# Two transformer blocks on one core: conditioning sums along rows of a transposed weight, the first activations in tiles of their own, the last output in three pieces

## The chip, the cores and the metric

The kernel runs on one core of a Trainium2 chip. The metric is the device time of one execution in microseconds (us). Comparisons are medians of several executions; one further execution is taken with the hardware profiler on, and all rows below come from it.

## What is computed

A sequence of 256 rows of width 1024 goes through a first block of two layers (feed-forward, mixer, feed-forward, each with a residual and a layer norm) and then through a second block of two layers, whose input and output are modulated by a conditioning vector `c`. Cut to what the change touches:

```
def swiglu_ffn(x, w_gu, w_down):
    a, u = jnp.split(x @ w_gu, 2, axis=-1)
    return (jax.nn.silu(a) * u) @ w_down

# second block, layer l; c is (1, 1024), w_ada[l] is (1024, 3072)
mod = jax.nn.silu(c) @ w_ada[l] + b_ada[l]
shift, scale, gate = jnp.split(mod, 3, axis=-1)
h = x * (1.0 + scale[:, None, :]) + shift[:, None, :]
...
x = layer_norm_2(ALPHA * x + (1.0 + gate[:, None, :]) * sub, ln_g[l], ln_b[l])
```

## The kernel before, in words

All matmuls work on fp32 numbers that are split into two parts: `hilo` (lines 375 to 378) and `get_at` (294 to 304) let ScalarE (ACT) write a rounded high part (`xx`, `whi`, `xhi`, `hth`) and VectorE (DVE) the rest as a low part (`wlo`, `xlo`, `htl`). A product then takes three matmuls, high by high, low by high and high by low.

The weights come from memory as a stream of pieces of 128 rows by up to 1024 columns, in the order in which `plan` (64 to 116) lists them. `load_piece` (280 to 286) issues each on the SP queue into one of six staging tiles `st` (NS = 6); a tile is free again when DVE has made the low part of its piece. The split pieces lie in eight pairs `whi`, `wlo` (NB = 8) or in tiles `xhi`, `xlo` of the stage. A stage's instructions are written in program order, and each engine runs its own list in order.

A feed-forward stage runs over 22 chunks of 128 hidden columns. `gu_T` (520 to 546) makes the gate and up products of a chunk: for each of 8 k tiles (128 rows of the weight) and both halves, one matmul of 512 columns with `whi` as weights and high and low activations side by side as moving data, and one of 256 columns with `wlo`: 16 such pairs a chunk. Even chunks write the two PSUM banks `mm`, odd chunks the two banks `tr`; DVE's additions at line 541 free the banks. `down` adds the product of chunk c - 6 to four banks `ac`.

The start of the kernel is special. `setup` clears part of `x` and `warm` (222 to 229) runs 18 matmuls on it. The first feed-forward takes its activations transposed from memory in four pieces of two k tiles (`load_xT`, 231 to 236), which go through the same staging tiles and the same SP queue as the weights, between the pieces of chunk 0 (`FIRST_K`, line 27). The identity `idn` for transposes is loaded by the POOL queue.

The modulation is worked out beside the feed-forward stages. 48 pieces of `w_ada` lie in the stream, eight for each of six groups of 1024 outputs (`ADA`, line 30: one group in the first, two in the second, two in the third, one in the fourth feed-forward stage). In `ada_step` (306 to 327) a piece holds 128 inputs on partitions and 1024 outputs on columns. DVE multiplies it by the partition's `silu(c)` and adds it to `ada` (lines 315 and 317). After the eighth piece the partitions still have to be summed: TensorE transposes `ada` in two groups of four blocks of 128 columns (`transposes`, 441 to 447) into a bank `tr`, and DVE sums each group along its rows (line 324).

At the end `ln` (400 to 429) writes each half of 128 rows in two pieces of 512 columns, both issued on SP.

Of the kernel before, what the change touches and what calls it, by code (L numbers as in the profile page):

```python
# [17 lines left out]
D = 1024  # L18
# [8 lines left out]
FIRST_K = ((0, 1), (1, 1), (2, 2), (4, 2), (6, 2))  # L27
# [36 lines left out]
def plan(take):  # L64
# [6 lines left out]
    def ffn(i, l):  # L71
# [47 lines left out]
def lay_out(inp):  # L119
    d = {}  # L120
    f = lambda a: np.ascontiguousarray(a)
    src = {**inp, "w_ukv": np.concatenate([inp["w_uk_2"], inp["w_uv_2"]], 2), "w_out_2": inp["w_out_2"][:, Y2]}
# [7 lines left out]
    d["xT"] = f(inp["x"][0].T.reshape(4, 2, 128, 2, 128).transpose(0, 2, 3, 1, 4).reshape(4, 128, 512))  # L130
    d["bada"] = f(inp["b_ada_2"].reshape(DEPTH * 24, 128).T)
    d["c"] = f(inp["c_2"].reshape(8, 128).T)
# [50 lines left out]
class Kernel:  # L183
# [12 lines left out]
    def setup(self):  # L196
# [9 lines left out]
        self.c = self.const.tile([128, 8], F32, name="c")  # L206
        self.sc = self.const.tile([128, 8], F32, name="sc")
        self.mod = [self.const.tile([128, 24], F32, name=f"mod{l}") for l in range(DEPTH)]
        nc.gpsimd.dma_start(out=self.idn, in_=d["idn"])
# [4 lines left out]
        nc.scalar.activation(out=self.sc, in_=self.mhalf, func=AF.Silu)  # L214
# [4 lines left out]
        self.n_ox = 0  # L219
        self.warm()  # L220
# [10 lines left out]
    def load_xT(self, q):  # L231

        st = self.stage.tile([128, 1024], F32, name="st")[:, :512]
        self.nc.sync.dma_start(out=st, in_=self.d["xT"][q])
        ks = slice(2 * q, 2 * q + 2)
        self.hilo(self.xh[:, :, ks, :], self.xl[:, :, ks, :], st.rearrange("p (t k n) -> p t k n", t=2, k=2))

    def load_x(self, c):

        if c == 7:  # L240
# [5 lines left out]
            self.nc.sync.dma_start(out=self.c, in_=self.d["c"])  # L246
            self.nc.scalar.activation(out=self.sc, in_=self.c, func=AF.Silu)
# [6 lines left out]
    def open_block1(self):  # L254
# [5 lines left out]
        self.dec = p.tile([128, 2048], F32, name="dec")  # L260

# [44 lines left out]
    def ada_step(self, pool):  # L306

        nc = self.nc
        while self.pieces and self.pieces[0][0] == "a":
            _, l, k, _, cols = self.pieces[0][3]  # L310
            st = self.load_piece()[1]
            c = self.sc[:, k:k + 1]
            if k == 0:
# [1084 lines left out]
```

## Time and profile before

| | |
|---|---|
| time, median of three runs | 1345.4 us (1343.68 to 1346.33) |
| the profiled execution, its own time | 1350.96 us |
| span in that profile, first to last instruction | 1349.2 us |
| matmuls, TensorE busy | 7654, 1319.8 us (98%) |
| VectorE busy, ScalarE busy | 1031.4 us (76%), 741.4 us (55%) |
| moved by DMA | 262.88 MB |

PE is TensorE's matmuls, DVE is VectorE, ACT is ScalarE, SPq is the queue on which SP issues DMAs. Times of rows count from the span's start. A busy PE is not PE at its peak, since matmuls are pipelined: what a group of them costs is read from start to start. In a timeline row the first number is the start, the second the time that the row covers, `x4` the number of instructions in it, and the bracket holds the idle time before it and who ended that. `PEclk` is the granted clock of TensorE.

### The profile page before, as it was taken

To read this page: it belongs to the slowest core of one execution; us is meant where nothing else is said; L and a number is where in the kernel's file an instruction comes from. 1 tells how busy PE (TensorE), PEld (TensorE's weight loads), DVE (VectorE), ACT (ScalarE), POOL (GpSimd) and SP (SyncE) were. 2 spreads that over 40 slices of the span, in tenths; PEclk is the share of its full clock that TensorE was granted. 3 is DMA by queue.
4 is the path that set the end of the run, shared out by engine and by line. 5 is a ranking of instruction groups with operands and counts; after the bars stand their busy time and mean duration, and the time that the engine had idled before them with its cause. 6 is when DMAs were issued, how large, how long until landed. Compare 5 with 4: busy or idle time off the path is not lost. (4 is left out here: it accounts for less than half of the span.)

```text
span 1349.2 us, 20437 instructions
## 1 busy us (share of the span) xinstructions
PE 1319.8 (98%) x7654; PEld 1135.5 (84%) x7654; DVE 1031.4 (76%) x1713; ACT 741.4 (55%) x1310; POOL 25.8 (2%) x35
## 2 busy tenths in 40 slices
PE   8999999999999999999999999999999999999997
PEld 6888888788887888888887878888889998799886
DVE  6876769968977669787579878687585797866976
ACT  6654536446655546545446456555355678456681
POOL 0000000010000000000000110000000000000000
PEclk9999999999999999999999999999999999999999
DMA  8987724546878628877423637677445433464420
GB/s 290 332 297 234 240 93 133 203 134 232 316 244 268 212 83 305 299 255 250 156 96 125 252 124 269 202 260 265 131 151 184 154 126 128 138 203 160 143 77 32
DMA packets 75235, 262.88 MB, mean 195 GB/s; under 512 B 9168, under 2 KB 9552, under 8 KB 75008
## 3 DMA queue, kind: packets, MB, share of 16 engines
q1 hardware_dynamic: 74592, 259.82, 56.9%
q0 software_dynamic: 544, 1.75, 0.4%
q8 instruction: 60, 0.98, 0.3%
q14 instruction: 39, 0.32, 0.1%
HBM read 260.49 MB, written 1.05 MB: 194 GB/s over the span
## 5 line engine op out<-in xcount | busy, mean ns | idle before, releaser
L302 DVE TENSOR_TENSOR wlo<-st,whi 128x1024 fp32r<-128x1024 f32 (+4 forms) x319 | 372.3, 1176 | 74.6 <-ACT whi L300 73.1
L300 ACT ACTIVATE whi<-st 128x1024 fp32r<-128x1024 f32 (+4 forms) x319 | 322.6, 1021 | 123.4 <-PE mm L331 49.6
L331 PE MATMUL mm<-xx,whi 128*128 128x256 f32 (+1 forms) x1296 | 335.0, 334 | 1.2 <-DVE xx L378 1.2
L331 PE MATMUL mm<-xx,wlo 128*128 128x256 f32 x928 | 262.1, 283 | 0.0
L331 PEld LDWEIGHTS mm<-xx,whi 128*128 128x128 f32 x1296 | 221.0, 191 | 25.7 <-ACT whi L300 1.5
L331 PE MATMUL mm<-whi,xx 128*128 128x512 f32 (+3 forms) x744 | 219.1, 372 | 0.6 <-DVE xx L378 0.4
L331 PE MATMUL tr<-xx,whi 128*128 128x512 f32 x560 | 197.3, 394 | 2.2 <-ACT whi L300 2.2
L331 PEld LDWEIGHTS mm<-xx,wlo 128*128 128x128 f32 x928 | 176.8, 191 | 2.2 <-DVE wlo L302 0.5
L331 PE MATMUL tr<-xx,wlo 128*128 128x256 f32 x560 | 157.6, 282 | 0.5 <-DVE wlo L302 0.5
L331 PEld LDWEIGHTS mm<-whi,xx 128*128 128x128 f32 x744 | 135.0, 188 | 24.5 <-issue 1.6
L302 DVE TENSOR_TENSOR xlo<-st,xhi 128x1024 fp32r<-128x1024 f32 x106 | 128.4, 1219 | 26.0 <-ACT xhi L300 26.0
L300 ACT ACTIVATE xhi<-st 128x1024 fp32r<-128x1024 f32 x106 | 110.2, 1056 | 67.6 <-PE ac L331 56.3
L331 PE MATMUL mm<-wlo,xx 128*128 128x512 f32 (+3 forms) x372 | 137.0, 369 | 0.0
L331 PEld LDWEIGHTS tr<-xx,whi 128*128 128x128 f32 x560 | 105.4, 188 | 26.0 <-ACT whi L300 2.6
L331 PE MATMUL ac<-xlo,hth 128*128 128x512 f32 x320 | 126.2, 394 | 0.0
L331 PE MATMUL ac<-xhi,hth 128*128 128x512 f32 x320 | 125.4, 392 | 0.0
L331 PEld LDWEIGHTS tr<-xx,wlo 128*128 128x128 f32 x560 | 106.5, 190 | 2.2 <-DVE wlo L302 1.0
L331 PE MATMUL ac<-xhi,htl 128*128 128x512 f32 x320 | 105.0, 392 | 0.0
L317 DVE SCALAR_TENSOR_TENSOR ada<-st,sc,ada 128x1024 f32<-128x1024 f32 x42 | 53.8, 1281 | 41.5 <-DMA st<-in_w 41.5
L331 PEld LDWEIGHTS mm<-wlo,xx 128*128 128x128 f32 x372 | 70.1, 188 | 10.6 <-issue 0.3
L331 PEld LDWEIGHTS ac<-xhi,hth 128*128 128x128 f32 x320 | 60.1, 188 | 14.1
L331 PEld LDWEIGHTS ac<-xhi,htl 128*128 128x128 f32 x320 | 60.0, 188 | 12.4
(275 smaller groups left out, 1823.1 us busy)
## 6 DMA issues: line engine op xcount, KB each, us to landing
st<-in_w SPq DMA_DIRECT2D x442, 512.0 KB, 4.6
st<-in_w SPq DMA_DIRECT2D x20, 384.0 KB, 3.7
g<-in_lng SPq DMA_DIRECT2D x8, 512.0 KB, 4.8
b<-in_lnb SPq DMA_DIRECT2D x8, 512.0 KB, 5.2
st<-in_w SPq DMA_DIRECT2D x8, 432.0 KB, 4.1
st<-in_w SPq DMA_DIRECT2D x8, 296.0 KB, 3.9
st<-in_xT SPq DMA_DIRECT2D x4, 256.0 KB, 4.5
x<-in_x SPq DMA_DIRECT2D x2, 512.0 KB, 7.7
```

Source lines behind the costliest of these rows:

```text
L300: nc.scalar.activation(out=hi[:, :m], in_=st[:, :m], func=AF.Copy)
L302: nc.vector.tensor_tensor(out=lo[:, :m], in0=st[:, :m], in1=hi[:, :m].bitcast(F32), op=ALU.subtract)
L317: nc.vector.scalar_tensor_tensor(out=self.ada, in0=st, scalar=c, in1=self.ada, op0=ALU.mult, op1=ALU.add)
L331: return self.nc.tensor.matmul(*a, **k).ins
```

## The change

There are four edits.

1. `w_ada` is laid out transposed. A piece now holds 128 outputs on partitions and all 1024 inputs on columns. `silu(c)` is spread over all partitions as a tile `sc` of 128 by 1024. One DVE instruction for each piece multiplies and sums along the row (`accum_out`) straight into a column of `mod`. The products and transposes on TensorE, the tile `ada` and the sums at line 324 are gone. The 48 pieces stay where they were in the stream.
2. The activations `xx` are laid out by k tile, for each k the 256 high columns and then the 256 low ones (`xk`). The first activations no longer go through staging tiles: they land in `x[1]`, in the upper half of `x[0]` and in a temporary tile. The first piece is issued in two halves of one k tile on the ACT queue, ahead of everything else on it; the other three stay on SP.
3. Chunk 1 takes its weights in three pieces (2, 2 and 4 k tiles) in place of two. `idn` and the broadcast `c` (512 KB) are loaded on SP behind chunk 7, with `x`.
4. The last output is written in pieces of 512, 384 and 128 columns; the middle one is issued on the ACT queue.

```diff
-FIRST_K = ((0, 1), (1, 1), (2, 2), (4, 2), (6, 2))
+FIRST_K = (((0, 1), (1, 1), (2, 2), (4, 2), (6, 2)), ((0, 2), (2, 2), (4, 4)))
...
-            for k, kk in FIRST_K if start and c == 0 else ((0, 4), (4, 4)):
+            for k, kk in FIRST_K[c] if start and c < 2 else ((0, 4), (4, 4)):
...
-                yield piece("a", "w_ada_2", al, k, 1, rng(1024 * q, 1024))
+                yield piece("a", "w_ada_T", al, 8 * q + k, 1, rng(0, 1024))
...
-        nc.gpsimd.dma_start(out=self.idn, in_=d["idn"])
...
-        self.xx = self.xt.tile([128, 2, 2, 8, 128], F32R, name="xx")
-        self.xh, self.xl = self.xx[:, 0], self.xx[:, 1]
-        self.xhl = self.xx.rearrange("p e t k n -> p (e t) k n")
+        self.xk = self.xt.tile([128, 8, 512], F32R, name="xx")
+        self.xh, self.xl = (self.xk[:, :, c:c + 256].rearrange("p k (t n) -> p t k n", t=2) for c in (0, 256))
...
+        self.xw = self.tmp()
+        for k in range(2):
+            nc.scalar.dma_start(out=self.x[1][:, 256 * k:256 * k + 256], in_=d["xT"][0][:, 256 * k:256 * k + 256])
...
-    def load_xT(self, q):
-        st = self.stage.tile([128, 1024], F32, name="st")[:, :512]
-        self.nc.sync.dma_start(out=st, in_=self.d["xT"][q])
-        ks = slice(2 * q, 2 * q + 2)
-        self.hilo(self.xh[:, :, ks, :], self.xl[:, :, ks, :], st.rearrange("p (t k n) -> p t k n", t=2, k=2))
+    def load_xT(self, k, n):
+        q, r = divmod(k, 2)
+        src = (self.x[1][:, 0:512], self.x[1][:, 512:], self.x[0][:, 512:], self.xw)[q][:, 256 * r:256 * (r + n)]
+        if q > 0:
+            self.nc.sync.dma_start(out=src, in_=self.d["xT"][q])
+        self.hilo(self.xk[:, k:k + n, :256], self.xk[:, k:k + n, 256:], src.rearrange("p (k n) -> p k n", k=n))
...
-            self.nc.sync.dma_start(out=self.c, in_=self.d["c"])
-            self.nc.scalar.activation(out=self.sc, in_=self.c, func=AF.Silu)
+            self.nc.sync.dma_start(out=self.idn, in_=self.d["idn"])
+            self.nc.sync.dma_start(out=self.sc, in_=self.d["c"].to_broadcast([128, D]))
+            self.nc.scalar.activation(out=self.sc, in_=self.sc, func=AF.Silu)
...
-            if k == 0:
-                self.ada = pool.tile([128, 1024], F32, tag="ada", name="ada", bufs=2)
-                nc.vector.tensor_scalar(out=self.ada, in0=st, scalar1=c, scalar2=None, op0=ALU.mult)
-            else:
-                nc.vector.scalar_tensor_tensor(out=self.ada, in0=st, scalar=c, in1=self.ada, op0=ALU.mult, op1=ALU.add)
-            if k < 7:
+            nc.vector.scalar_tensor_tensor(out=st, in0=st, scalar=1.0, in1=self.sc, op0=ALU.mult, op1=ALU.mult,
+                                           accum_out=self.mod[l][:, j:j + 1])
+            if j % 8 < 7:
                 continue
...
-            for h in range(2):
-                ps = self.transposes([self.ada[:, 512 * h + 128 * i:512 * h + 128 * i + 128] for i in range(4)])
-                nc.vector.tensor_reduce(out=m[:, 4 * h:4 * h + 4], in_=ps.rearrange("p (k n) -> p k n", k=4), axis=AX.X,
-                                        op=ALU.add)
...
-            for c0, c1 in HALVES:
+            for c0, c1, q in ((0, 512, nc.sync), (512, 896, nc.scalar), (896, 1024, nc.sync)):
                 nc.vector.scalar_tensor_tensor(out=x[:, c0:c1], in0=x[:, c0:c1], scalar=y, in1=self.b[:, c0:c1],
                                                op0=ALU.mult, op1=ALU.add)
-                nc.sync.dma_start(out=self.out[128 * t:128 * t + 128, c0:c1], in_=x[:, c0:c1])
+                q.dma_start(out=self.out[128 * t:128 * t + 128, c0:c1], in_=x[:, c0:c1])
...
-                    K.mm(o, lhsT=hi[:, i, cs], rhs=K.xhl[:, :, k, :], start=k == 0, stop=False, skip_group_check=True)
+                    K.mm(ps[j], lhsT=hi[:, i, cs], rhs=K.xk[:, k, :], start=k == 0, stop=False, skip_group_check=True)
```

What the edits do to the order of the instructions shows at three places. On SP, the first issues of the kernel before (`in_xT` the transposed activations, `in_w` the weight stream, `st` a staging tile):

```order
L234 DMA st<-in_xT 128x512
L284 DMA st<-in_w 128x256 x2
L234 DMA st<-in_xT 128x512
L284 DMA st<-in_w 128x512
L234 DMA st<-in_xT 128x512
L284 DMA st<-in_w 128x512
L234 DMA st<-in_xT 128x512
L284 DMA st<-in_w 128x512
L284 DMA st<-in_w 128x1024 x15
```

The same place of the changed kernel:

```order
L288 DMA st<-in_w 128x256 x2
L237 DMA x_80<-in_xT 128x512
L288 DMA st<-in_w 128x512
L237 DMA x_79<-in_xT 128x512
L288 DMA st<-in_w 128x512
L237 DMA tmp<-in_xT 128x512
L288 DMA st<-in_w 128x512 x3
L288 DMA st<-in_w 128x1024 x14
```

The weights of chunk 0 stand first, no `in_xT` goes to a staging tile, and the last `128x512 x3` is chunk 0's last piece with chunk 1's first two.

On ACT, from its start to the first PSUM reads of chunk 0 (`sa<-mm`, `su<-mm`), before:

```order
L214 ACT_TABLE_LOAD
L214 ACTIVATE sc<-mhalf 128x8
L377 ACTIVATE xx<-st 128x2x256
...
L377 ACTIVATE xx<-st 128x2x256
L300 ACTIVATE whi<-st 128x512
L300 ACTIVATE whi<-st 128x1024
L540 ACTIVATE sa<-mm 128x256
L540 ACTIVATE su<-mm 128x256
L300 ACTIVATE whi<-st 128x1024
```

The same place of the changed kernel:

```order
L219 DMA x_80<-in_xT 128x256 x2
L220 ACT_TABLE_LOAD
L220 ACTIVATE one<-mhalf 128x8
L373 ACTIVATE xx<-x_80 128x256
...
L373 ACTIVATE xx<-tmp 128x2x256
L304 ACTIVATE whi<-st 128x512 x3
L535 ACTIVATE sa<-mm 128x256
L535 ACTIVATE su<-mm 128x256
L304 ACTIVATE whi<-st 128x1024
```

ACT issues the first activations itself, and two pieces of chunk 1 (half of its weights) are split ahead of `sa<-mm`; the other half follows behind `su<-mm`, as before.

On PE, behind the last chunk of the first feed-forward stage (`ac` are the down products, `tr<-idn,ada` the transposes), before:

```order
L331 MATMUL tr<-xx,wlo 128x256
L331 MATMUL ac<-xhi,hth 128x512
L331 MATMUL ac<-xlo,hth 128x512
L331 MATMUL ac<-xhi,hth 128x512
L446 MATMUL tr<-idn,ada 128x128 x4
L331 MATMUL ac<-xlo,hth 128x512
L331 MATMUL ac<-xhi,htl 128x512 x2
L331 MATMUL ac<-xhi,hth 128x512
L446 MATMUL tr<-idn,ada 128x128 x4
L331 MATMUL ac<-xlo,hth 128x512
```

The same place of the changed kernel:

```order
L327 MATMUL tr<-xx,wlo 128x256
L327 MATMUL ac<-xhi,hth 128x512
L327 MATMUL ac<-xlo,hth 128x512
L327 MATMUL ac<-xhi,hth 128x512
L327 MATMUL ac<-xlo,hth 128x512
L327 MATMUL ac<-xhi,htl 128x512 x2
```

The transposes are gone, and the matmuls around them stand in their order. The same holds at the five other places.

## Rows read from the trace of the kernel before

**Rows 1.** The page, part 1: busy us, share of the span, instructions.
```profile
PE 1319.8 (98%) x7654; PEld 1135.5 (84%) x7654; DVE 1031.4 (76%) x1713; ACT 741.4 (55%) x1310; POOL 25.8 (2%) x35
```
**Rows 2.** Waits of PE: engine line waited for: us in total, times, longest.
```profile
PE tr L446 <- DVE sa L541: 3.3, 2, 2.0
```
**Rows 3.** Windows: length, busy us of PE, PEld, DVE, ACT, POOL, PEclk, DMA share, GB/s.
```profile
0.00:23.20 23.20, 18.14 (x83) 13.85 (x84) 12.89 (x20) 13.05 (x21) 0.91 (x5) 0.93 0.86 291
...
6.00:7.00 1.00, 1.00 (x7) 0.75 (x5) 0.00 (x0) 0.19 (x1) 0.00 (x0) 1.00 1.07 412
...
17.00:18.00 1.00, 1.00 (x4) 0.89 (x4) 1.00 (x2) 1.00 (x2) 0.00 (x0) 0.50 1.03 418
```
**Rows 4.** Timeline of the start: start, us, engine, line, operation.
```profile
1.09 4.02 PE L331 MATMUL tr<-x 128*128 128x256 bf16 x18 [1.09 <-DVE x L225]
...
4.99 1.19 PE L331 MATMUL mm<-xx,whi 128*128 128x512 f32 x2
...
6.81 0.63 ACT L377 ACTIVATE xx<-st 128x512 fp32r<-128x512 f32 x1 [1.45 <-DMA st<-in_xT]
...
8.19 1.68 SPq L284 DMA_DIRECT2D st<-in_w  x3
...
8.31 0.71 PE L331 MATMUL mm<-xx,whi 128*128 128x512 f32 x2 [1.19 <-DVE xx L378]
...
10.29 0.63 ACT L300 ACTIVATE whi<-st 128x512 fp32r<-128x512 f32 x1
...
12.63 0.27 PE L331 MATMUL mm<-xx,wlo 128*128 128x256 f32 x1
...
14.05 1.06 ACT L300 ACTIVATE whi<-st 128x1024 fp32r<-128x1024 f32 x1 [3.12 <-DMA st<-in_w]
...
15.16 0.73 PE L331 MATMUL tr<-xx,whi 128*128 128x512 f32 x2 [2.25 <-ACT whi L300]
...
22.80 0.40 PE L331 MATMUL tr<-xx,whi 128*128 128x512 f32 x1
...
23.16 0.40 PE L331 MATMUL mm<-xx,whi 128*128 128x512 f32 x1
```
**Rows 5.** Timeline of PE at the first and the last group of transposes.
```profile
176.59 0.39 PE L331 MATMUL ac<-xhi,hth 128*128 128x512 f32 x1
176.92 0.66 PE L446 MATMUL tr<-idn,ada 128*128 128x128 f32 x4
177.34 0.48 PE L331 MATMUL ac<-xlo,hth 128*128 128x512 f32 x1
...
966.34 0.40 PE L331 MATMUL ac<-xhi,hth 128*128 128x512 f32 x1
...
967.01 0.47 PE L331 MATMUL ac<-xlo,hth 128*128 128x512 f32 x1
```
**Rows 6.** Timeline of PE at a group of transposes that waits for long.
```profile
407.05 0.40 PE L331 MATMUL ac<-xhi,htl 128*128 128x512 f32 x1
...
409.48 0.65 PE L446 MATMUL tr<-idn,ada 128*128 128x128 f32 x4 [2.03 <-DVE sa L541]
409.89 0.47 PE L331 MATMUL ac<-xhi,htl 128*128 128x512 f32 x1
```
**Rows 7.** Groups of DVE by form: xcount, busy us, mean ns, idle before.
```profile
L317 DVE SCALAR_TENSOR_TENSOR ada<-st,sc,ada 128x1024 f32<-128x1024 f32 x42 | 53.8, 1281 | 41.5 <-DMA st<-in_w 41.5
...
L324 DVE TENSOR_REDUCE mod<-tr 128x4 f32<-128x512 f32 x12 | 8.2, 687 | 2.7 <-PE tr L446 2.7
```
**Rows 8.** Windows again: six chunks of the second feed-forward stage.
```profile
425.91:475.79 49.88, 49.88 (x266) 42.87 (x265) 31.85 (x43) 25.08 (x42) 0.00 (x0) 1.00 0.65 219
```
**Rows 9.** The last output: DVE's timeline row; landing of its four DMAs.
```profile
1344.18 1.41 DVE L422 SCALAR_TENSOR_TENSOR x<-x,rs_y,b 128x512 f32<-128x512 f32 x2
...
DMA to landing us min/median/max: 2.0/2.1/2.1
```
**Rows 10.** Timeline of ACT behind chunk 7's loads.
```profile
45.69 0.39 ACT L540 ACTIVATE sa<-tr 128x256 f32<-128x256 f32 x1 [2.32 <-PE tr L331]
```

More of the change, by code (lines that the diff above doesn't have):

```diff
@@ L121, in lay_out @@
     f = lambda a: np.ascontiguousarray(a)
-    src = {**inp, "w_ukv": np.concatenate([inp["w_uk_2"], inp["w_uv_2"]], 2), "w_out_2": inp["w_out_2"][:, Y2]}
+    src = {**inp, "w_ukv": np.concatenate([inp["w_uk_2"], inp["w_uv_2"]], 2), "w_out_2": inp["w_out_2"][:, Y2],
+           "w_ada_T": inp["w_ada_2"].transpose(0, 2, 1)}
     def take(name, l, k0, kk, cols):
@@ L129, in lay_out @@
     d["x"] = f(inp["x"][0])
-    d["xT"] = f(inp["x"][0].T.reshape(4, 2, 128, 2, 128).transpose(0, 2, 3, 1, 4).reshape(4, 128, 512))
+    d["xT"] = f(inp["x"][0].T.reshape(4, 2, 128, S).transpose(0, 2, 1, 3).reshape(4, 128, 512))
     d["bada"] = f(inp["b_ada_2"].reshape(DEPTH * 24, 128).T)
-    d["c"] = f(inp["c_2"].reshape(8, 128).T)
+    d["c"] = f(inp["c_2"].reshape(1, D))
     d["lng"] = f(np.stack([inp["ln1_g"], inp["ln2_g"], inp["ln3_g"], inp["ln_g_2"]]).reshape(4, DEPTH, 1, D))
@@ L205, in setup @@
         self.idn = self.const.tile([128, 128], F32, name="idn")
-        self.c = self.const.tile([128, 8], F32, name="c")
-        self.sc = self.const.tile([128, 8], F32, name="sc")
+        self.one = self.const.tile([128, 8], F32, name="one")
         self.mod = [self.const.tile([128, 24], F32, name=f"mod{l}") for l in range(DEPTH)]
-        nc.gpsimd.dma_start(out=self.idn, in_=d["idn"])
         self.gc = self.const.tile([128, 64], F32, name="gc")
@@ L213, in setup @@
         nc.vector.memset(self.mhalf, -0.5)
-        nc.scalar.activation(out=self.sc, in_=self.mhalf, func=AF.Silu)
-        self.xx = self.xt.tile([128, 2, 2, 8, 128], F32R, name="xx")
-        self.xh, self.xl = self.xx[:, 0], self.xx[:, 1]
-        self.xhl = self.xx.rearrange("p e t k n -> p (e t) k n")
+        self.xk = self.xt.tile([128, 8, 512], F32R, name="xx")
+        self.xh, self.xl = (self.xk[:, :, c:c + 256].rearrange("p k (t n) -> p t k n", t=2) for c in (0, 256))
         self.xT, self.yT = {}, {}
         self.n_ox = 0
+        self.xw = self.tmp()
+        for k in range(2):
+            nc.scalar.dma_start(out=self.x[1][:, 256 * k:256 * k + 256], in_=d["xT"][0][:, 256 * k:256 * k + 256])
+        nc.scalar.activation(out=self.one, in_=self.mhalf, func=AF.Silu)
         self.warm()
@@ L260, in open_block1 @@
         self.dec = p.tile([128, 2048], F32, name="dec")
+        self.sc = p.tile([128, D], F32, name="sc")
     def close_block1(self):
@@ L531, in gu_T @@
                     cs = slice(128 * j, 128 * j + 128)
-                    o = ps[j].rearrange("p (a n) -> p a n", a=4)
-                    K.mm(o, lhsT=hi[:, i, cs], rhs=K.xhl[:, :, k, :], start=k == 0, stop=False, skip_group_check=True)
-                    K.mm(o[:, 0:2, :], lhsT=lo[:, i, cs], rhs=K.xh[:, :, k, :], start=False, stop=k == 7,
+                    K.mm(ps[j], lhsT=hi[:, i, cs], rhs=K.xk[:, k, :], start=k == 0, stop=False, skip_group_check=True)
+                    K.mm(ps[j][:, :256], lhsT=lo[:, i, cs], rhs=K.xk[:, k, :256], start=False, stop=k == 7,
                          skip_group_check=True)
@@ L566, in body @@
             pcs = []
-            for q in range(4):
-                K.load_xT(q)
-                pcs += K.get(1 if q else 2)
+            for k, n in FIRST_K[0]:
+                K.load_xT(k, n)
+                pcs += K.get(1)
             self.gu_T(0, pcs)
@@ L572, in body @@
         for c in range(1 if self.start else 4, NCH):
-            self.gu_T(c, K.get(2))
+            self.gu_T(c, K.get(3 if self.start and c == 1 else 2))
             if c in (7, 13, 15) and self.start:
@@ L576, in body @@
             with K.tc.issue_after(last):
-                K.ada_step(self.fp)
+                K.ada_step()
             if c == 11:
```

7 lines of the change are left out of this document (3 added, 4 removed).

## The prediction

> **What bounds the kernel now.** I read the page first: PE is busy 98% of the span, DVE 76%, ACT 55% [rows 1]. A share of busy time is an average, so the next views are the waits of PE and the windows, to see where PE is really the limit. In six chunks of the second feed-forward stage PE is busy in all of 49.88 us, DVE in 31.85 [rows 8]: there PE is the bound, and every matmul that goes away shortens the stage. The windows show the place where PE is not the bound: of the first 23.2 us it is busy only 18.14 [rows 3]. And the list of waits holds one that this change touches: transposes of line 446 waited 3.3 us in two pieces for DVE's line 541, which frees a bank `tr` [rows 2]. So I work out three places: the six groups of conditioning sums, the start, the end.
>
> **The conditioning sums: what PE no longer does.** At the first group the reader is to see a detour [rows 5]: a down product starts at 176.59, four transposes at 176.92, the next down product at 177.34. Such a product holds PE for 0.23 us (a pair of 512 and 256 columns takes 0.36 from 22.80 to 23.16 [rows 4], two thirds of it is 0.24), so the detour costs 177.34 - 176.59 - 0.23 = 0.52. At the last one it is 967.01 - 966.34 - 0.23 = 0.44. There are twelve such groups of four; without their long waits they lie between 0.36 and 0.52, and I take 12 x 0.475 = 5.7. Two of the twelve also wait: the one at 409.48 for 2.03 us, since DVE, busy with other work, had not yet freed the bank [rows 6]; there PE goes from 407.05 to 409.89 for one matmul. Both waits together are the 3.3 of the list [rows 2]. The down products behind the transposes need neither the bank nor DVE's sum, so without transposes PE has nothing to wait for there: the next user of those banks is the next odd chunk, more than 5 us later. Sum: 5.7 + 3.3 = 9.0 us. All of it lies in feed-forward stages, where PE is the bound and its last matmul starts the layer norm, so I count all of it. Bounds: 5.7 if the two waits come back at another place, 9.5 above.
>
> **The same sums on DVE.** Before, a group of eight pieces took one tensor by scalar, seven instructions of 1281 ns and two sums of 687 ns [rows 7]. Now it takes eight with a sum along the row, a form that the trace does not show on DVE. Below it stands the same form without the sum, 1.28 us. Above it stands that form with a separate pass over 1024 columns, 1.28 + 2 x 0.69 = 2.65. I take 1.4, near the lower end, since the sum needs no second reading of data. In six chunks DVE has 49.88 - 31.85 = 18 us to spare and six such instructions [rows 8]; even 2.65 adds only 8.2. The cover is that spare time, and the in-order wait for the piece stays (41.5 us of DVE idle before line 317 are spent on its DMA [rows 7]). Cost: nothing.
>
> **The start: what goes missing now.** Four places in the timeline [rows 4]. The first product starts at 4.99, when the 18 warming matmuls end (1.09 + 4.02 = 5.11 by the modelled end). PE stops until 8.31 for activations whose DMA landed at 6.81, and then runs through chunk 0 to 12.90. There it stops again: the first weights of chunk 1 land at 14.05, because their DMA was issued at 8.19, when DVE had given back a staging tile. PE resumes at 15.16, and for a while at the lower clock (granted 0.50 at 17 to 18 [rows 3], the level of 1.2 GHz; before the fall it had idled 2.25 us). Chunk 2 starts at 23.16. A chunk at the upper level takes 16 pairs of 0.35 to 0.36, 5.65 us. So between 12.90 and 23.16 the hole is 10.26 - 5.65 = 4.6 us.
>
> **The start: what the change does there.** The activations no longer take staging tiles, so the six tiles reach to chunk 1, and its first two pieces are issued as soon as earlier DMAs land, some 3 to 4 us before 8.19. They come behind 2 MB of chunk 0, whose last piece had landed when ACT split it at 10.29. At the 412 GB/s of a full window [rows 3], 256 KB take 0.64 us: landings near 10.9 and 11.6, both split before PE needs them. The third piece (512 KB) lands between 12.9 at that rate and 15.8 at two thirds of it with the issue late. Its split stands behind `sa<-mm` on ACT, 1.06 us for the high part and about 1.3 for the low one (as a DVE form of that width in [rows 7]); PE comes to it 2.8 us into chunk 1, at 15.5. I take a landing near 14, high part at 15.1, low part at 16.4, and 0.5 us of waiting. Chunk 0 itself ends where its second activations land: the same 512 KB are ahead of them, their issue is one place earlier, and the load of `idn` is gone. I take 0.2 us earlier (0 to 0.5). The first product stays at 5.0, since the warming matmuls are unchanged. With PE busy I expect the granted clock to stay at 1.00. Sum: 4.6 - 0.5 + 0.2 = 4.3 us, bounds 2.3 (third piece at 15.8, chunk 1 ends near 20.9) and 5.1 (no wait, chunk 0 0.5 earlier).
>
> **Edits with one answer.** The moving data of the 512-column matmul now lie in one run and not in four. The products of `down`, which read one run, cover 0.39 us a row just as those of `gu_T` cover 0.40 [rows 4, 5]; no change. The loads of `idn` and the broadcast `c` add 576 KB behind chunk 7, 1.4 us of DMA at 412 GB/s. ACT's Silu behind them grows to about 1 us (1.06 for a copy of that width [rows 4]) and may wait for the landing; behind it ACT idles 2.32 us before PE's next chunk is ready [rows 10], which covers both. If that cover were gone, one such wait would cost 1 to 2 us once.
>
> **The end.** Two pieces of 512 columns take DVE 1.41 us [rows 9]; three pieces add one start, about 0.07. The last DMA, 64 KB in place of 256 KB, was 2.1 us from issue to landing. If the fixed part stays and 192 KB less move at 412 GB/s, it ends 0.45 earlier, but the middle piece, issued 0.2 before it, sets a bound. I take 0.2 us gained, with -0.5 to +0.3 as bounds.
>
> **The sum.** 9.0 + 4.3 + 0.2 = 13.5 us. The profiled execution takes 1350.96 us (span 1349.2), which gives 1337.5; it stands 5.6 us above the median of the runs, 1345.4. The savings are stretches of fixed length, so I take them off the median: 1331.9.
>
> **Rivals.**
>
> *Only the issue time is gained at the start.* The DMAs share one set of engines. If the early weights take their bandwidth from the activations of chunk 0, the second activations land later, the gap before 8.31 grows by what the one at 12.90 loses, and the clock may fall as before. For it: of the 2 MB of chunk 0 little landed before 6.81. Against it: in order, nothing that is new stands ahead of these activations. Then the start brings about 0.9 us, two issues on SP, the total is 10.1, and the time 1335.3. The Trainium skill, "DMA: Bandwidth & Descriptors", section "Issuing engines are not separate DMA queues", says that DMAs issued on several engines interleave on the same 16 engines and that only the sequencer's time to issue is saved. By that rule the move of the first piece to ACT alone is worth this little; the trace of before, with nearly all loads on one queue, does not show it either way.
>
> *PE's freed time is lost again.* The stages end on PE, but what follows may be late: weights of the next stage, or DVE, which was late at 409.48. Then half of the 9.0 stays: 13.5 - 4.5 = 9.0, 1336.4; with a poor start too, 1340. Against it: PE has no wait for weights in these stages among its list.
>
> *Nothing that can be measured.* Start and end shift but the first stages wait for something else as long as before: within 0.2% of 1345.4.
>
> *Slower: the summing instruction makes DVE the bound.* Its place is every chunk with a conditioning piece. A chunk lasts 8.31 us (49.88 / 6) and DVE works 5.31 in it [rows 8]; DVE overtakes PE when the instruction takes more than 1.28 + 3.0 = 4.3 us. From there each further us costs 48 us. At 4.7 us it would be 48 x 0.4 = 19 us lost against 13.5 gained, 1351. For it: the form is not in the trace. Against it: it would have to take over three times its sister form. The Trainium skill, "Vector Engine (DVE) Microarchitecture Reference", section 7, "Points that are easy to get wrong", says that this instruction with two non-bf16 sources in SBUF runs at half throughput, as both read ports are taken and none is left for reading back the accumulator. If that doubles the 1.28 of line 317, which already reads two such sources, it gives 2.56, under the 4.3: the sum stays, and it is the reason why I leave this rival more than 1 in 100.
>
> **How the numbers follow.** The forecast, 12 to 15 us gained: 0.62. Poor start: 0.15 (1334 to 1337). Freed time lost: 0.09 (1336 to 1341). More than 15 gained, as the first stages start with more weights in hand: 0.03. Nothing measurable: 0.07. Slower: 0.04. A measurement of this kernel tells 0.2%, 2.7 us, from no change; all gains above are faster than 1342.7, so faster 0.89, same 0.07, slower 0.04. The range takes in the forecast with its bounds, the poor start and most of the third: 1328.5 to 1338.5.
>
> **What would show it.** Right: no transposes fed from the conditioning sums; the distance across each of the six places 0.9 to 3 us shorter; chunk 2 starting at 18.5 to 19.5 in place of 23.16; the granted clock 1.00 throughout the first 24 us; the new DVE form at 1.3 to 1.5 us. Wrong: a gap of more than 1 us before the second activations or in chunk 1; the new DVE form above 2.6 us; new waits of PE for weights late in the feed-forward stages; a wait at the layer norms as long as what was saved before them.

## The result, and the profile after

The changed kernel takes **1329.9 us** (median of 4 runs, 1329.1 to 1330.3) beside 1345.9 for the kernel before, measured together with it (4 runs, 1343.7 to 1346.8): ratio 0.9883, 95% interval 0.9866 to 0.9900. That is 16.0 us gained; the prediction was 13.5 and 1331.9. The profiled execution of the changed kernel takes 1329.58 us (span 1327.8).

The page of the changed kernel, part 1 (busy us, share of the span, instructions), answers to [rows 1]:

```profile
PE 1308.1 (99%) x7606; PEld 1128.1 (85%) x7606; DVE 1022.9 (77%) x1753; ACT 741.2 (56%) x1312; POOL 25.2 (2%) x34
```

PE has 48 matmuls less and is busy 11.7 us less, while the span is 21.4 us shorter: the rest was waiting. The list of PE's waits (engine, line, waited for: us in total, times, longest) no longer has the transposes that stood for DVE's `sa` [rows 2]; it now begins with

```profile
PE ac L327 <- ACT PT L687: 1.9, 4, 0.5
```

At the place of [rows 6], PE's timeline of the changed kernel shows what the stretch is without transposes:

```profile
398.93 0.39 PE L327 MATMUL ac<-xhi,hth 128*128 128x512 f32 x1
399.15 0.39 PE L327 MATMUL ac<-xlo,hth 128*128 128x512 f32 x1
399.38 0.62 PE L327 MATMUL ac<-xhi,htl 128*128 128x512 f32 x2
399.85 0.40 PE L327 MATMUL ac<-xhi,hth 128*128 128x512 f32 x1
```

Four down products in 0.92 us, 0.23 each, where 407.05 to 409.89 went by for one of them before. DVE is no earlier than it was: its sum stands at 400.35 and its split of a weight at 401.49, and only then, at 402.63, does it come to `sa` (409.01 before). Nothing on PE needs that bank in this stretch now.

The new form on DVE, all instructions of line 316 (min/median/max ns):

```profile
L316 DVE SCALAR_TENSOR_TENSOR st<-st,sc x48: 1210/1224/1229, 81.7 to 912.1; 128x1024 f32<-128x1024 f32 x48
L316 DVE DVE_READ_ACCUMULATOR st<-st,sc x48: 76/82/85, 82.8 to 913.2; 128x1 f32 x48
```

One sum is a pass of 1.22 us and a second, short instruction of 0.08 that reads the accumulator: 1.30 together, against the 1281 ns of the old form [rows 7]. The subtraction that splits the weights, of the same width and types, stands on the page (group: busy us, mean ns of one, idle before) with

```profile
L306 DVE TENSOR_TENSOR xlo<-st,xhi 128x1024 fp32r<-128x1024 f32 x106 | 128.4, 1218 | 18.8 <-ACT xhi L304 18.1
```

At the start, PE, ACT and SP of the changed kernel (a piece of each engine's timeline, to hold beside [rows 4]; the row of SP begins with the third piece of chunk 1):

```profile
4.76 0.78 PE L327 MATMUL mm<-xx,whi 128*128 128x512 f32 x1
...
12.09 0.40 PE L327 MATMUL tr<-xx,whi 128*128 128x512 f32 x1
...
17.70 0.40 PE L327 MATMUL mm<-xx,whi 128*128 128x512 f32 x1
```

```profile
5.73 0.63 ACT L373 ACTIVATE xx<-x 128x512 fp32r<-128x512 f32 x1 [0.65 <-DMA x<-in_xT]
...
12.57 1.05 ACT L304 ACTIVATE whi<-st 128x1024 fp32r<-128x1024 f32 x1
```

```profile
5.79 2.74 SPq L288 DMA_DIRECT2D st<-in_w  x2
```

SP has issued all weights of chunk 1 before 8.19, where the kernel before issued its first ones. Chunk 1 follows chunk 0 without a gap, its third piece (12.57) is split without having waited for a DMA, and chunk 2 begins at 17.70 in place of 23.16. The granted clock doesn't fall, and the window writes it as 1.00; what the trace holds of it begins only at 7.12 us (see the last section):

```profile
0.00:18.60 18.60, 17.49 (x87) 14.03 (x88) 12.75 (x23) 13.31 (x24) 0.20 (x4) 1.00 0.89 333
```

### The profile page after: what moved, and what is told of

Same layout as the page of the kernel before. It is cut to its first block, busy times and chain, and to the rows that moved or that the text cites. A ratio compares the mean times of both kernels' runs of the same rounds, so it can differ in the third digit from the quotient of the medians.

```text
span 1327.8 us, 20378 instructions
## 1 busy us (share of the span) xinstructions
PE 1308.1 (99%) x7606; PEld 1128.1 (85%) x7606; DVE 1022.9 (77%) x1753; ACT 741.2 (56%) x1312; POOL 25.2 (2%) x34
## 5 line engine op out<-in xcount | busy, mean ns | idle before, releaser
L306 DVE TENSOR_TENSOR wlo<-st,whi 128x1024 fp32r<-128x1024 f32 (+5 forms) x320 | 372.3, 1174 | 66.6 <-ACT whi L304 66.3
L304 ACT ACTIVATE whi<-st 128x1024 fp32r<-128x1024 f32 (+5 forms) x320 | 322.8, 1018 | 115.3 <-DMA st<-in_w 45.7
L316 DVE SCALAR_TENSOR_TENSOR st<-st,sc 128x1024 f32<-128x1024 f32 x48 | 58.6, 1222 | 53.2 <-DMA st<-in_w 53.1
L373 ACT ACTIVATE hth<-sa 128x256 fp32r<-128x256 f32 x76 | 31.4, 413 | 79.1 <-DVE sa L538 79.0
```

Of the source, the lines that this page charges most:

```text
L304: nc.scalar.activation(out=hi[:, :m], in_=st[:, :m], func=AF.Copy)
L306: nc.vector.tensor_tensor(out=lo[:, :m], in0=st[:, :m], in1=hi[:, :m].bitcast(F32), op=ALU.subtract)
L316: nc.vector.scalar_tensor_tensor(out=st, in0=st, scalar=1.0, in1=self.sc, op0=ALU.mult, op1=ALU.mult, accum_out=self.mod[l][:, j:j + 1])
L373: nc.scalar.activation(out=hi, in_=src, func=AF.Copy)
```

## The experiments

The traces are compared by one table. Each layer norm starts with a `BATCH_NORM_AGGREGATE` on DVE, and the distance from the last one of a stage to the first of the next is that stage's length. The first row is the start of chunk 2, the second the way from there to the first layer norm. Places 1 to 6 are the six groups of eight pieces whose sums were made by transposes. One trace each; the last row is read to 0.05. "Again" and "again 2" are two more executions of the kernel before; "idle" is the changed kernel with transposes that nobody reads, into the banks `tr` or `mm`. The edits follow below.

| us | before | again | again 2 | sums alone | changed | all but sums | idle, `tr` | idle, `mm` |
|---|---|---|---|---|---|---|---|---|
| start of chunk 2 | 23.16 | 19.78 | 20.19 | 19.64 | 17.70 | 17.34 | 19.03 | 17.48 |
| to first norm (place 1) | 166.79 | 166.79 | 166.78 | 165.09 | 165.09 | 166.23 | 166.18 | 166.50 |
| feed-forward 2 (2, 3) | 180.18 | 183.75 | 179.33 | 175.84 | 175.86 | 178.96 | 180.08 | 177.57 |
| feed-forward 3 (4, 5) | 179.43 | 179.93 | 179.55 | 175.85 | 175.86 | 179.08 | 179.57 | 177.62 |
| second mixer | 101.95 | 99.18 | 99.47 | 100.32 | 99.42 | 99.53 | 99.03 | 99.41 |
| feed-forward 4 (6) | 176.99 | 176.98 | 176.99 | 175.86 | 175.87 | 177.04 | 176.94 | 176.75 |
| last mixer | 166.37 | 166.46 | 164.52 | 164.03 | 164.51 | 164.61 | 166.29 | 166.04 |
| last norm to end | 6.71 | 6.71 | 6.67 | 6.91 | 7.01 | 6.85 | 6.96 | 6.95 |

### The sums alone, and all but the sums

The kernel before with the sums alone:

```diff
-                yield piece("a", "w_ada_2", al, k, 1, rng(1024 * q, 1024))
+                yield piece("a", "w_ada_T", al, 8 * q + k, 1, rng(0, 1024))
...
+            nc.vector.scalar_tensor_tensor(out=st, in0=st, scalar=1.0, in1=self.sc, op0=ALU.mult, op1=ALU.mult,
+                                           accum_out=self.mod[l][:, j:j + 1])
```

> The kernel before with the conditioning sums alone changed (transposed weight, sum along rows on DVE, broadcast c; start, layout and end as before). Theory, from the marks of the two traces (six places shorter by 1.1, 3.2, 1.05, 2.45, 1.1 and 1.1 us): 10.1 us gained, 1335 to 1337 beside 1345.9. The forecast's own sum, 9.0, gives 1336.9. Rival (PE's freed time is half lost again): 4.5 gained, 1341.4.

Measured: 1332.6 (1331.7 to 1333.4), 13.5 gained beside 1346.15 (ratio 0.9897, 0.9883 to 0.9911). That is more than any of the three.

The changed kernel with the same lines put back:

> The changed kernel with the conditioning sums put back as they were (transposes on PE, columns of c). What is left is the start, the layout and the end. Theory, from the marks (chunk 2 starts 5.5 us earlier, end 0.3 later): 5 to 5.7 gained, 1340.2 to 1340.9, and chunk 2 at 17.7 in its trace. The forecast's 4.3 + 0.2 gives 1341.4. Rival (only the time of issues is gained at the start): 0.9 gained, 1345.

Measured: 1342.0 (1339.0 to 1343.1), 4.1 gained (ratio 0.9965, 0.9952 to 0.9979): near the forecast's 4.5, in an interval of 2.8 to 6.5. Its chunk 2 starts at 17.34. The two gains add up to 17.6, 1.6 more than the whole; both are taken from 18 runs of the kernel before that lie between 1343.3 and 1349.1.

The table says where the sums' gain lies. In the kernel with the sums alone feed-forward 2, 3 and 4 last 175.84 to 175.86, as in the changed kernel, so the sums make the whole difference in these stages: against "again 2" the changed kernel is 3.5, 3.7 and 1.1 shorter there, and 1.1 at place 1 (1.7 in the row, 0.55 of it in chunks 2 to 6, see the last section): 9.4 in all. The trace of the kernel with the sums alone is 9.9 us shorter than that of "again 2" (1330.8, 1340.7); the other part of its 13.5 is that the median beside it, 1346.15, stands 3.7 above "again 2" (1342.47).

### What the transposes cost on PE

The changed kernel with 48 transposes put back that read a constant and that nobody reads:

```diff
+            for h in range(2):
+                self.transposes([self.idn] * 4)
```

> The changed kernel with the 48 transposes put back on PE alone: they read the constant idn, write the same banks tr as before, and nothing reads them; the sums stay on DVE in the new form. Theory (all that was gained at the six places was PE's own detours, 6.7, and the wait for the bank, 3.4): about 10 us lost against the changed kernel, 1340. Forecast's sum: 9.0 lost, 1339. Rival (part of the gain came from DVE's shorter work, not from PE): 5.7 lost or less, 1335.6.

and the same into the banks `mm`:

> As the kernel with the 48 idle transposes, but they write banks mm, which were freed a chunk earlier. Theory: the wait of 3.4 belongs to the banks tr, so only the detours are left: 6 to 6.7 us lost against the changed kernel, 1336 to 1336.6, with no wait of these transposes for DVE in the trace. Rival (the wait is one for DVE in any bank): the same loss as with banks tr, 1340.

Measured: 1343.6 (1341.6 to 1347.2, 12 runs) with banks `tr`, 13.7 above the changed kernel; 1335.6 (1335.2 to 1338.0, 6 runs) with `mm`, 5.7 above it. With banks `tr` the idle transposes alone cost as much as the new sums had gained (13.5), so that gain came from PE and not from the work of DVE. In `mm` they cost 5.7, which is the forecast's 12 x 0.475 (5.2 at the six places of its trace, without the 0.55 of chunks 2 to 6), and what the banks add is 8.0, not the 3.4 of the waits in the trace. The timelines of PE at the place of [rows 6], `tr` and then `mm`:

```profile
402.07 0.40 PE L329 MATMUL ac<-xhi,htl 128*128 128x512 f32 x1
404.50 0.66 PE L444 MATMUL tr<-idn 128*128 128x128 f32 x4 [2.03 <-DVE sa L538]
404.91 0.48 PE L329 MATMUL ac<-xhi,htl 128*128 128x512 f32 x1
```

```profile
400.39 1.03 PE L444 MATMUL mm<-idn 128*128 128x128 f32 x8
401.18 0.48 PE L329 MATMUL ac<-xhi,hth 128*128 128x512 f32 x1
401.49 0.40 PE L329 MATMUL ac<-xlo,hth 128*128 128x512 f32 x1
```

With `tr` the wait is there although the transposes depend on no sum: it is the bank's. With `mm` there is none, so rival and wait are told apart; the theory's 10 us stand in the trace as well (the four feed-forward stages are 1.1, 4.2, 3.7 and 1.1 longer than the changed kernel's). What the medians have on top is the subject of the next part.

### The kernel before, twice more

> The kernel before, unchanged, for a second trace. Theory A (the start before differs between executions, since the kernel that changed only the sums started chunk 2 at 19.64 with the same first loads): chunk 2 at 19 to 22 here, and the start's part of the gain is 2 to 4 us, not the 5.5 between the two first traces. Theory B (the start before always stands as in the first trace): chunk 2 at 23 again. In the second mixers: falls of the granted clock like those of the first trace (at 709 and 1286 us) in some executions and not in others.

> The kernel before a third time, to see whether the start of chunk 2 and the falls of the granted clock in the mixers change from one execution to the next. Theory A: chunk 2 within 19 to 23.2 but not where the first two traces have it; Theory B: at 23 each time.

Measured: 1348.3 and 1342.5; 13 other runs of this kernel, taken with these, lie between 1342.4 and 1349.0. Theory A holds: chunk 2 at 19.78 and 20.19. The first trace, from which the prediction was read, had the worst start of the three. PE's waits there, "again" first, then "again 2":

```profile
14.48 0.51 PE L331 MATMUL tr<-xx,wlo 128*128 128x256 f32 x2 [0.52 <-DVE wlo L302]
...
19.78 0.40 PE L331 MATMUL mm<-xx,whi 128*128 128x512 f32 x1
```

```profile
13.65 0.73 PE L331 MATMUL tr<-xx,whi 128*128 128x512 f32 x2 [0.38 <-ACT whi L300]
14.91 0.50 PE L331 MATMUL tr<-xx,wlo 128*128 128x256 f32 x2 [0.53 <-DVE wlo L302]
```

In place of the 2.25 us of [rows 4], a stop of 0.38 or none ahead of chunk 1, and no fall of the clock behind it.

The wait for the bank changes too: 3.3 us in the first trace, 4.6 and 2.7 in these. In "again" it did more than wait. PE's timeline and the windows from 404 to 414 (length, busy of PE, PEld, DVE, ACT, POOL, granted clock, DMA share, GB/s):

```profile
406.98 1.12 PE L446 MATMUL tr<-idn,ada 128*128 128x128 f32 x4 [2.90 <-DVE sa L541]
```

```profile
404.00:406.00 2.00, 0.07 (x1) 0.00 (x0) 2.00 (x3) 0.54 (x2) 0.00 (x0) 1.00 0.97 311
406.00:408.00 2.00, 1.02 (x5) 1.02 (x6) 2.00 (x4) 0.42 (x1) 0.00 (x0) 0.52 0.88 277
408.00:410.00 2.00, 2.00 (x6) 1.44 (x6) 1.32 (x4) 0.42 (x1) 0.00 (x0) 0.50 1.02 391
410.00:412.00 2.00, 2.00 (x8) 1.78 (x7) 0.88 (x2) 0.03 (x1) 0.00 (x0) 0.50 1.01 412
412.00:414.00 2.00, 2.00 (x10) 1.67 (x10) 2.00 (x4) 1.03 (x1) 0.00 (x0) 0.77 0.26 107
```

PE stood still, and for the next 6 us and more the granted clock was 0.50, the level of 1.2 GHz. The stage took 183.75 in place of 179.33: 1.6 of the 4.4 us is the longer wait, the other 2.8 the clock.

The same happens in the last mixer, where a wait that looks unrelated changes with the conditioning sums. ACT and PE, "before", then the changed kernel:

```profile
1283.29 1.06 ACT L300 ACTIVATE qiTw<-st 128x1024 fp32r<-128x1024 f32 x1 [2.31 <-DMA st<-in_w]
1284.26 0.81 ACT L1042 ACTIVATE y<-ac 128x128 f32<-128x128 f32 x3
...
1284.73 0.76 PE L331 MATMUL ac<-kbT,qbT 64*128 64x128 f32 x4 [1.54 <-ACT y L1042]
```

```profile
1262.97 1.06 ACT L304 ACTIVATE qiTw<-st 128x1024 fp32r<-128x1024 f32 x1 [1.43 <-DMA st<-in_w]
1263.94 0.80 ACT L1037 ACTIVATE y<-ac 128x128 f32<-128x128 f32 x3
...
1264.42 0.76 PE L327 MATMUL ac<-kbT,qbT 64*128 64x128 f32 x4 [0.66 <-ACT y L1037]
```

ACT waits for a weight, in order ahead of the copy `y` that PE needs. In the eight traces without the detours on PE (changed, sums alone, the four variants of start and end, the sum three and five times) PE waits 0.20 to 0.66 us here; in the six with them (of sums or idle) 1.23 to 1.66. In four of those six, and in none of the eight, the clock falls right behind. The windows behind it, before, then changed:

```profile
1286.00:1288.00 2.00, 2.00 (x10) 2.00 (x10) 2.00 (x9) 2.00 (x9) 0.00 (x0) 0.51 0.57 209
```

```profile
1266.00:1268.00 2.00, 2.00 (x19) 2.00 (x18) 2.00 (x8) 1.54 (x7) 0.00 (x0) 1.00 0.75 244
```

In 2 us PE does 10 instructions at the one clock and 19 at the other. The last mixer takes 166.4 us with a fall and 164.5 in "again 2", which waited 1.23 there and had none: 1.9, of which the longer wait is 0.3. (With the idle transposes in `mm` PE waited the same 1.23, and the clock fell.) In the second mixer of the first trace a fall and the wait of 2.01 ahead of it cost 2.5 together. "Again 2" has no fall between its start and its end, and it is among the fastest runs of the kernel before.

A mean granted clock is known for every run, not only for the profiled ones. Of the 38 runs of the kernel before that were taken with the experiments, eight have a mean of 0.994 or 0.995, and they take 1347.24 to 1349.13; the other 30, at 0.996 to 0.998, all take less, 1342.37 to 1347.15. So runs with more of the lower clock are the slow end of the scatter. It isn't all of it: the six at 0.998, the value of "again 2", have a median of 1343.9, beside 1344.8 for all 38.

### The start

The first activations on SP again:

```diff
-            nc.scalar.dma_start(out=self.x[1][:, 256 * k:256 * k + 256], in_=d["xT"][0][:, 256 * k:256 * k + 256])
+            nc.sync.dma_start(out=self.x[1][:, 256 * k:256 * k + 256], in_=d["xT"][0][:, 256 * k:256 * k + 256])
```

> The changed kernel with one edit: the first two pieces of x are issued on SP ahead of the first weights, not on ACT. Theory (what the second queue brings is the time of two issues, 0.43 to 0.45 us each): second activations land at about 6.6 in place of 5.73, chunk 2 starts at about 18.5 in place of 17.70, 0.9 us lost, 1330.8. Rival 1 (the DMA engines are shared, so the order of issue on queues does not matter): no change, 17.7. Rival 2 (the later activations open the gap again and the clock falls behind it): 2 us or more lost, chunk 2 at 20 or later.

All activations through the staging tiles again, on SP:

```diff
...
+        if r == 0:
+            self.xst = self.stage.tile([128, 1024], F32, name="st")[:, :512]
+            self.nc.sync.dma_start(out=self.xst, in_=self.d["xT"][q])
+        src = self.xst[:, 256 * r:256 * (r + n)]
...
```

> The changed kernel with the activations through the staging tiles again, all on SP (layout by k tile, the three pieces of chunk 1 and the late loads stay). Theory (the six staging tiles are what held back chunk 1): the DMA of chunk 1's weights waits again for a tile, PE has a gap before chunk 1 of 0.7 to 2.3 us, chunk 2 starts at 19.5 to 21.5, 1.8 to 4 us lost, 1331.7 to 1334. Rival (own tiles do nothing, the smaller pieces and the second queue closed the hole): 0.9 lost for the issues, chunk 2 at 18.6, no gap before chunk 1.

Chunk 1 in two pieces again:

```diff
-FIRST_K = (((0, 1), (1, 1), (2, 2), (4, 2), (6, 2)), ((0, 2), (2, 2), (4, 4)))
+FIRST_K = (((0, 1), (1, 1), (2, 2), (4, 2), (6, 2)), ((0, 4), (4, 4)))
```

> The changed kernel with chunk 1's weights in two pieces of 512 KB, as before, in place of three. Theory (the early issue closed the hole, the smaller pieces only smooth it): the first piece is split 0 to 0.6 us after PE could begin, chunk 2 at 17.7 to 18.3, at most 0.6 lost, 1330 to 1330.5. Rival (the small pieces closed the hole): a gap of over 1 us before or in chunk 1, 1.5 us or more lost.

Chunk 2 on PE, and the row behind which time was lost, of these three in turn:

```profile
5.52 0.63 ACT L373 ACTIVATE xx<-x 128x512 fp32r<-128x512 f32 x1 [0.29 <-DMA x<-in_xT]
...
17.75 0.40 PE L327 MATMUL mm<-xx,whi 128*128 128x512 f32 x1
```

```profile
9.15 2.85 SPq L286 DMA_DIRECT2D st<-in_w  x4
...
14.60 1.06 ACT L302 ACTIVATE whi<-st 128x1024 fp32r<-128x1024 f32 x1 [1.29 <-DMA st<-in_w]
...
19.43 0.40 PE L325 MATMUL mm<-xx,whi 128*128 128x512 f32 x1
```

```profile
13.79 0.50 PE L327 MATMUL tr<-xx,wlo 128*128 128x256 f32 x2 [0.41 <-DVE wlo L306]
...
19.00 0.39 PE L327 MATMUL mm<-xx,whi 128*128 128x512 f32 x1
```

*On SP*: 1330.5 (1330.1 to 1332.2). The second activations land at 5.52, no later than with two queues (5.73), and chunk 2 starts at 17.75: by the trace the first rival was right, the second queue brings nothing here. The rule of the Trainium skill ("DMA: Bandwidth & Descriptors", "Issuing engines are not separate DMA queues") agrees; even the time of two issues that it leaves is not to be seen in the trace. The median is 0.6 higher; the trace has that 0.6 in chunks 2 to 6 (last section), not in the loads.

*Staged*: 1331.8 (1330.8 to 1332.2), chunk 2 at 19.43. The third piece of chunk 1 comes late for want of a tile (issued at 9.15 in place of 5.79, split at 14.60 after a wait for its DMA; 12.57 and no such wait in the changed kernel): the theory, though PE now waits inside chunk 1 and not ahead of it. The kernel to compare with is *on SP*, which has the same queue: 1.7 us in the traces (17.75), 1.3 in the medians. Not all of the 1.7 is distinct from chance. Seven traces with the changed start (changed, all but sums, both idle ones, old end, the sum three and five times) begin chunk 2 between 17.34 and 19.03, and what differs among them lies ahead of chunk 1. Chunk 1 itself lasts 5.56 to 5.61 us in all seven and 5.59 on SP; staged it lasts 6.70. These 1.1 us stand clear of that scatter.

*Two pieces*: 1330.5 (1329.8 to 1331.0), chunk 2 at 19.00. The median lost 0.6, the theory's bound; the trace 1.3 at chunk 2, of which 0.7 were lost before chunk 1 began (12.76 in place of 12.09), where the edit changes nothing. Chunk 1 lasts 6.24, 0.6 more than the others' 5.6. The rival, 1.5 or more, falls.

### The end

```diff
-            for c0, c1, q in ((0, 512, nc.sync), (512, 896, nc.scalar), (896, 1024, nc.sync)):
+            for c0, c1, q in ((0, 512, nc.sync), (512, 1024, nc.sync)):
```

> The changed kernel with the last output in two halves on SP, as before. Read from the trace, since it is small: from the last BATCH_NORM_AGGREGATE to the end of the span, 7.0 us in the changed kernel and 6.7 in the one before. Theory (three pieces cost DVE one more start, and a small DMA lands no sooner): 6.7, 0.3 gained, 1329.6. The forecast's step (0.2 gained by the small last piece): 7.2, 0.2 lost, 1330.1.

Measured: 1329.4 (1329.1 to 1329.8), and 7.07 us from the last `BATCH_NORM_AGGREGATE` to the end, not 6.7. The changed kernel, which differs by this edit alone, takes 7.01, and its median is 0.5 higher, with ranges that overlap: nothing gained, and no loss shown. Over all traces the old form takes 6.67 to 7.07 (five, the three of the kernel before the lowest), the new one 6.85 to 7.49 (nine). The last rows of the changed kernel, to hold beside [rows 9] (DVE; then KB and us from issue to landing):

```profile
1322.48 1.54 DVE L418 SCALAR_TENSOR_TENSOR x<-x,rs_y,b 128x512 f32<-128x512 f32 x3
```

```profile
out_x<-x SPq DMA_DIRECT2D x1, 256.0 KB, 2.1
out_x<-x ACTq DMA_DIRECT2D x1, 192.0 KB, 2.0
out_x<-x SPq DMA_DIRECT2D x1, 64.0 KB, 2.0
```

Three pieces take DVE 0.13 longer than two, and 64 KB land as late after their issue as 192 or 256.

### The summing instruction, three and five times

Three times; for five times it is `range(4)`:

```diff
...
+            for _ in range(2):
+                nc.vector.scalar_tensor_tensor(out=junk, in0=st, scalar=1.0, in1=self.sc, op0=ALU.mult, op1=ALU.mult,
+                                               accum_out=self.mod[l][:, j:j + 1])
```

> The changed kernel with the summing instruction of each of the 48 pieces issued three times (two results thrown away), 2 x 1.30 us more of DVE a chunk. Theory (from the prediction's rows: DVE works 5.3 us in a chunk of 8.31, so 5.3 + 2.6 = 7.9 is still covered by PE): less than 5 us lost, 1330 to 1335. Rival (DVE issues in order, so the splits of weights behind the sums come late and PE waits long before DVE is full): 10 to 50 us lost.

> The changed kernel with the summing instruction of each of the 48 pieces issued five times, 4 x 1.30 = 5.2 us more of DVE a chunk. Theory (the price of the rival in the prediction that ends slower: DVE is the bound from 4.3 us an instruction, and each further us costs 48): 5 x 1.30 = 6.5, (6.5 - 4.3) x 48 = 106 us lost, 1436, DVE busy throughout these chunks. Rival (DVE has work to spare elsewhere, the queue of staging tiles smooths it): less than 70 lost.

Measured: 1341.7 (1337.7 to 1345.1), 11.8 above the changed kernel, in the rival's range; and 1409.6 (1409.3 to 1410.9), 79.7 above it, between the theory's 106 and the rival's 70. Windows of 50 us in feed-forward 2, once, three times, five times:

```profile
400.00:450.00 50.00, 50.00 (x267) 42.97 (x266) 35.77 (x55) 25.12 (x43) 0.00 (x0) 1.00 0.76 267
```

```profile
400.00:450.00 50.00, 50.00 (x267) 42.95 (x266) 49.58 (x79) 24.73 (x39) 0.00 (x0) 1.00 0.77 251
```

```profile
400.00:450.00 50.00, 40.81 (x188) 31.16 (x188) 47.26 (x77) 20.84 (x32) 0.00 (x0) 0.95 0.54 177
```

With three, DVE is full (49.58) and PE still loses nothing in this stretch; it pays at the stages' ends, where PE waits for the last chunk's hidden activations `hth` (two waits, the longer 6.51 us, the shorter this one). On ACT the reads of that chunk's products stand behind splits of weights, the last of which had waited 1.62 and 0.97 us for its DMA. At both places the granted clock fell to 0.50:

```profile
474.87 0.50 PE L331 MATMUL ac<-xhi,hth 128*128 128x512 f32 x1 [3.30 <-ACT hth L377]
```

With five, PE falls to 40.81. So DVE begins to decide near three sums, 3.9 us, and not at 4.3: in this stretch DVE works 35.77 / 50 of a chunk's 8.31 us, 5.94, and not the 5.31 of [rows 8], which was read from six other chunks; that puts the point at 1.3 + 2.4 = 3.7 here. Beyond it 2.6 us more an instruction cost 67.9 us, 26 for each and not 48. The mechanism of that rival exists, its point was some 0.6 too high for these chunks and its price nearly twice too high; the real instruction, at 1.30, is far from it.

## Why the prediction was right, step by step

The time stood in the range, 2.0 us below the forecast and 1.4 above the range's lower end, and the sign and the mechanism of the two main terms were right. But 16.0 gained is more than the 12 to 15 that had a chance of 0.62. It falls to "more than 15", which had 0.03, and no trace shows the reason given there. The parts were less good than the sum. The pair to compare is "again 2" (1342.5) and the changed kernel (1329.6), since neither has a fall of the clock between its start and its end. Their spans differ by 12.9 us, which lies in the 12 to 15:

| term | forecast | this pair | what the runs show |
|---|---|---|---|
| six places of sums | 9.0 | 9.4 | 5.7 for the matmuls alone (idle transposes in `mm`), 2.7 in the list of waits; the remaining 1.0 stands in no list |
| start | 4.3 | 3.0 | 1.6 ahead of chunk 1, 0.9 in it, 0.5 in chunks 2 to 6 |
| mixers | 0 | 0.8 | all in the first one, 99.96 and 99.06; it lies between 98.85 and 100.05 in the fourteen traces |
| end | 0.2 | -0.3 | not distinct from 0 |
| beyond this pair | 0 | none | 3.1 in the medians (16.0 - 12.9): the usual run of the kernel before is slower than "again 2" |

*The sums.* The mechanism was as told: PE no longer stops, DVE comes no sooner, nobody waits for it, and the freed time was not lost again: feed-forward 2, 3 and 4 last 175.86 us, each the same. The rival "PE's freed time is lost again" falls.

*The missing step.* The prediction counted a wait of PE at its length. In some executions the clock falls behind it, and the matmuls that follow pay once more: 2.8 us in "again" at this very place, 1.6 in the last mixer. Of the 3.1 us that the medians have beyond the pair some are such falls, since the slowest runs are those with the lowest mean clock; how many, no run tells. The four runs of the changed kernel differ by 1.2 us, the four of the kernel before that were taken with them by 3.1, its 38 runs beside the experiments by 6.8.

*The start.* Its mechanism was right: staging tiles held back chunk 1, and with them free there is no gap (staged: 1.1 us in chunk 1, up to 1.7 with what lies ahead of it). The size of its terms was not. The hole of 4.6 was read from one execution, with a stop of 2.25 us and a fall of the clock behind it that three other starts of the same order ("again", "again 2", sums alone) don't have; in the pair the hole is 1.3, a stop of 0.38 and the 0.9 of chunk 1. The 5.5 between the two first traces, above the prediction's bounds, is that accident. The other term, chunk 0 ending 0.2 earlier, was too small: without the stop it ends 1.2 earlier in the pair, because its second activations land earlier: PE goes on with them at 8.68 and at 7.51, and from there chunk 0 takes 4.6 us in both. "Again 2" splits them on ACT at

```profile
7.18 0.63 ACT L377 ACTIVATE xx<-st 128x512 fp32r<-128x512 f32 x1 [0.86 <-DMA st<-in_xT]
```

and the changed kernel at 5.73. With staging tiles it is 6.29 to 7.18 (five traces), with own tiles 5.52 to 6.01 in eight traces and 7.48 in a ninth (idle, `tr`). Why they land earlier is open; it isn't the second queue. So chunk 2 came at 17.70, ahead of the 18.5 to 19.5 that were to show the prediction right. A start taken 1.3 us too large and the 3.1 beyond the pair taken as nothing stood against each other: that the time missed by no more than 2.0 was in part luck. The half microsecond of waiting for chunk 1's third piece that the prediction allowed did not come.

*The new form on DVE.* Forecast 1.4, measured 1.22 + 0.08. The Trainium skill ("Vector Engine (DVE) Microarchitecture Reference", section 7) says that this instruction with two non-bf16 sources in SBUF runs at half throughput and has no port left for reading the accumulator. Here it takes no longer than the subtraction of two sources of that width and type (line 306, 1.22 us), and reading the accumulator costs 82 ns. The trace of before also has a DVE instruction of that width with one such source (ns, as above):

```profile
L315 DVE TENSOR_SCALAR ada<-st,sc x6: 737/746/755, 84.2 to 865.3; 128x1024 f32<-128x1024 f32 x6
```

It takes 0.75 us. So two sources cost 1.6 to 1.7 times one, 1.22 to 1.28, with a sum or without, and the doubling that the prediction allowed for on top of 1.28 doesn't come.

*The end.* The step that failed: that a DMA of 64 KB lands 0.45 us sooner than one of 256 (by its own rate 192 KB are 0.48). It lands at the same 2.0 to 2.1. The third start on DVE took 0.13 and not 0.07.

*The profile above its median.* The forecast took the savings off the median, not off the profiled execution that stood 5.6 above it. That was right: that execution stands 8.5 above "again 2", and a poor start (3.0), the falls in the second and the last mixer (2.5 and 1.9) and longer waits in feed-forward 2 (0.9) are 8.3 of it. All of these vary.

What stays open: why the weight `qiTw` lands sooner in the last mixer once the detours are gone, what decides whether the clock falls behind a wait of some 1.2 to 2 us (the 2.03 of [rows 6] had no fall behind it, the 2.90 of "again" had; of two waits of 1.23 one had), why the second activations land earlier, and how the 3.1 us beyond the pair divide.

## What to carry to other kernels

Work that only passes a result through PE (transposes for a sum) costs more than its matmuls where it needs a PSUM bank that another engine frees: write it elsewhere, or into a bank that has been free for long. A wait of PE is worth its length and, in some executions, as much again for the clock behind it, so a kernel without such waits gains in its median and in its scatter. Before a stall at the start is priced, look at it in a second and third execution: chunk 2 here moved by 3.4 us between three runs of one kernel, and by 1.7 between seven traces with the changed start.

## What the runs showed of the hardware that was not expected

The first products of the changed kernel stand 0.64 us apart, those of chunk 2 0.35 (as in [rows 4]):

```profile
6.19 0.63 PE L327 MATMUL mm<-xx,whi 128*128 128x512 f32 x1
...
6.83 0.53 PE L327 MATMUL mm<-xx,whi 128*128 128x512 f32 x1
```

The window from 5.50 to 6.80 writes the granted clock as 1.00 all the same. This is a gap in the record, not half pace at the full clock: the trace's first entry of the granted clock, a 1.00, stands at 7.12 us, and a window counts what has no entry as 1.00. All fourteen traces have such a first entry, between 4.18 and 7.12 us, and in each PE's matmuls, the warming ones or the products, keep half pace ahead of it and full pace behind it. So a kernel here starts at the level of 1.2 GHz, and a window of its first 7 us says nothing of the clock. It did no harm: with the old end the entry stands at 5.11, PE does its first products at full pace, then waits 0.98 us for `whi` and goes on at 7.63; here it goes on at 7.51 without a wait.

Chunks 2 to 5 last 5.55 us each in eight traces (changed, sums alone, all but sums, idle `tr`, two pieces, old end, the sum three and five times) and 5.65 in six (the three of before, idle `mm`, first activations on SP, staged), with either layout of `x`; chunk 6 differs by some 0.1 as well, later ones don't (8.31 in all). It is 0.5 us in all, and nearly the whole of what the kernel with the activations on SP had lost in its trace by the first layer norm (0.6). The cause is open; the layout by k tile is not it.
